# A two-layer hybrid model: the first layer's first two projections on x laid out by features, and the values' projection moved to second place

## The chip, the cores and the metric

The kernel runs on one NeuronCore of a Trainium2 chip, as one program with one launch. The metric is the device time of one execution in microseconds (us), the median of several runs. TensorE (PE) multiplies matrices into PSUM, PEld is its loading of the stationary operand, VectorE (DVE), ScalarE (ACT) and GpSimd (POOL) work element by element, and SyncE (SP) issues all DMA transfers from one queue, in order. Each engine works through its own queue in the order in which the program was written out.

## What is computed

The input x has 256 tokens of 1024 features. It passes through two hybrid layers (`layer0`, `layer1`), then a SwiGLU block, a mixing block and another SwiGLU block, all with residual sums. The part that the change touches is the head of a hybrid layer:

```python
def rmsnorm(x, g):
    xf = x.astype(jnp.float32)
    y = xf * lax.rsqrt(jnp.mean(xf * xf, axis=-1, keepdims=True) + EPS)
    return (y * g.astype(jnp.float32)).astype(x.dtype)
...
    p = split_columns(rmsnorm(x, norm_g) @ w_in)
...
    dq = rmsnorm(heads(p['dsa_q'], DSA_HEADS), dsa_q_g)
    dk = rmsnorm(heads(p['dsa_k'], DSA_HEADS), dsa_k_g)
    iq = heads(p['idx_q'], IDX_HEADS) * (IDX_DIM ** -0.5)
    iw = p['idx_w'] * (IDX_HEADS ** -0.5)
    topk = min(TOPK_MAX, s // 4)
    hd = dsa_sparse_attention(dq, dk, heads(p['dsa_v'], DSA_HEADS), iq, p['idx_k'], iw, rel_bias, topk)
```

The sparse attention scores every key with the index projections (idx_q, idx_k, idx_w), keeps the 64 best keys of each query, and does softmax attention of four heads over them with a relative bias. Two other branches (an mLSTM and a gated linear attention) run beside it on other columns of the same projection, and one output projection joins the three. The norm's factor of a token is one number for its row, so it can be multiplied into a projection's result instead of into x; the gain g belongs to the feature, so it has to be in x or in the weights beforehand.

## The kernel before

All weights are read from DRAM in units of 128 x 1024 f32 (512 KB), in the order in which the program uses them (362 units). `fetch` loads a unit into `raw` (3 buffers), then ACT casts it to float32r (`hi`, line 123) and DVE computes the rest (`lo` = raw - hi, line 124); the pool `ws` holds 5 such pairs. A projection does three matmuls for each product: hi with x's high part, hi with x's low part, lo with x's high part (`mm3`, line 156). `proj_a` puts tokens on the partitions (512 columns, 4 units, 48 matmuls of 128x512), `proj_b` puts features there (units of 24 matmuls of 128x256).

A layer calls its projections in a fixed order: dq (queries), iq (index queries), misc (index keys, gates), dk (keys), gq and gk (linear attention), dv (values), dz (gate of the sparse attention), gv, mv, mo and so on. Between the units `tick` steps through jobs, generators that issue the other work in pieces: `dsa_select` makes the scores `sc` and takes the 64 best of them on DVE in eight rounds, and at its end (line 552) turns them into a penalty, which POOL adds to the bias `pen` (line 554, four adds). `join(select)` stands after dz, so that `dsa_attend` starts with gv: the logits `dl` on PE (line 597), `lg` on DVE (line 600: dl, scaled, plus `pen`), the softmax (lines 625 to 633), and four steps later the transposes `pTp` of the first 128 tokens' probabilities on PE (line 232). The scheduler then lays all instructions out engine by engine, with the weight splits given a priority ahead of the other work.

The program's start is separate (`run`): x is loaded with tokens on the partitions, `normed` computes the factor r of each token (ACT squares, DVE, POOL), DVE multiplies x by r and by the gain, PE transposes the result (`xT`), ACT and DVE split it into the high and low part, and the first dq matmul follows. Four matmuls on zeros (`warm`) stand before. Other constants are loaded behind the first weights, and a strip of the bias table goes to DRAM and back (`bias_build`).

```python
        self.load_x(0)
        self.xn, fill = self.norm(gains[stages[0]])
        self.load_x(1)
...
            turns[0]()
            first = self.weights()
            turns[1]()
```

Of the kernel before, what the change touches and what calls it, by code (L numbers as in the profile page):

```python
# [34 lines left out]
class Net:  # L35
    def __init__(self, ctx, tc, a, out, dbg=None):
# [9 lines left out]
        self.operands()  # L46
        self.gap(pool("mid"), 96)
        self.t2 = pool("t2", 7)
# [5 lines left out]
        self.unit = 0  # L54
        self.jobs, self.ready, self.pins = [], [], None
        self.consts()
# [94 lines left out]
    def mm3(self, out, w, x, swap, first, last):  # L151

        (wh, wl), (xh, xl) = w, x
        for i, (ww, xx) in enumerate(((wh, xh), (wh, xl), (wl, xh))):
            lhsT, rhs = (xx, ww) if swap else (ww, xx)
            self.nc.tensor.matmul(out, lhsT=lhsT, rhs=rhs, start=first and i == 0, stop=last and i == 2)  # L156

# [22 lines left out]
    def rows(self, ps, x, k0, first, last, toks, w):  # L180

        for k in range(2):
            ww = [z[:, 512 * k:512 * (k + 1)] for z in w]
            for t in toks:
                xs = [z[:, k0 + k, P * t:P * (t + 1)] for z in x]
                self.mm3(ps[t], ww, xs, True, first and k == 0, last and k == 1)

    def proj_b(self, x, name, n=2):
# [40 lines left out]
    def transposes(self, srcs, name):  # L229
        ps = self.bank([P, len(srcs), P], name)  # L230
        for i, s in enumerate(srcs):
            self.nc.tensor.transpose(ps[:, i, :], s, self.ident)
        return ps

    def consts(self):
        nc, a = self.nc, self.a
        self.x = self.big.tile([P, 2, D], F32, tag="x", name="x")
        nc.sync.dma_start(self.ident, a["ident"])
        self.mhalf = self.const.tile([P, 16], F32, tag="mhalf", name="mhalf")
        nc.gpsimd.memset(self.mhalf, -0.5)  # L240

    def load_x(self, t):
        self.nc.sync.dma_start(self.x[:, t, :], self.a["x"][P * t:P * (t + 1)])

    def warm(self):

        nc = self.nc
        w = self.tmp([P, 512], "warm")
        nc.vector.memset(w, 0.0)
# [10 lines left out]
    def loads(self):  # L260
        nc = self.nc
        self.cols = self.held("cols")
# [3 lines left out]
        self.ones = self.const.tile([4, S], F32, tag="ones", name="ones")  # L266
        nc.gpsimd.memset(self.ones, 1.0)
# [17 lines left out]

    def norm(self, g_src):


        g = self.row_bc(g_src, D, "g_bc")
        self.x2 = self.big.tile([P, KT, 2, S], F32R, tag="x2", name="x2")  # L290
# [22 lines left out]
    def normed(self, t, g):  # L313
# [4 lines left out]
        sq = [nc.scalar.activation(xs[h], self.x[:, t, 512 * h:512 * (h + 1)], AF.Square, scale=1.0 / 32, accum_out=ss[:, h:h + 1]) for h in range(2)]  # L318
        r = self.small([P, 1], "r")
        nc.vector.scalar_tensor_tensor(r, ss[:, 0:1], EPS, ss[:, 1:2], ALU.add, ALU.add)  # L320
# [64 lines left out]


    def bias_build(self):

        nc, a = self.nc, self.a
        tab = self.tmp([32, 4], "tab")  # L390
        nc.sync.dma_start(tab, a["rel_bias"])
        hot = self.tmp([32, 512], "hot")
        nc.sync.dma_start(hot, a["hot"])
        yield
        yield
        ps = self.bank([4, 512], "strip")
# [11 lines left out]
    def layer(self, l):  # L408
        nc, a = self.nc, self.a
        x = self.xn  # L410
        yh = self.work([P, 16, S], "yh", dtype=F32R)
        yl = self.work([P, 16, S], "yl", dtype=F32R)
        self.y = (yh, yl)

        qs = self.t4([P, 2, 512], "qs")
# [41 lines left out]
        nc.gpsimd.memset(v1[:, :, :, 256:257], 1.0)  # L457
        hp = self.work([P, 2, D], "hp")

# [17 lines left out]

        gbc = self.row_bc(a["ml_norm_g"][l], D, "mlg")

        def zs(u, need):  # L480
# [13 lines left out]
        self.join(scores)  # L494
        self.start(self.gla_out(gvs, srg))
        h1 = head(1)
        outs(1)
# [66 lines left out]

    def dsa_q(self, t, ps, qs, qT, rq):
        nc = self.nc
        nc.scalar.copy(qs[:, t, :], ps)
        self.head_rms(ps.rearrange("p (h d) -> p h d", h=4), rq[:, t, :], 1.0 / 128, 128 ** -0.5)
# [504 lines left out]
    def run(self, stages):  # L1073
        a = self.a
        gains = {"layer0": a["norm_g"][0], "layer1": a["norm_g"][1], "ffn1": a["ffn1_norm_2"], "mix": a["mix_norm_2"], "ffn2": a["ffn2_norm_2"]}
        self.load_x(0)
        self.xn, fill = self.norm(gains[stages[0]])
        self.load_x(1)
        self.floor = self.tc.cur_priority
        self.warm()  # L1080
        with self.tc.manual_schedule(engines={mybir.EngineType.Activation, mybir.EngineType.DVE}):
            turns = [fill(t) for t in range(2)]
            turns[0]()
            first = self.weights()
            turns[1]()
        self.ready = [first]
        self.turn = None
        self.loads()
        self.start(self.bias_build())
# [42 lines left out]
def layouts(np, ins):  # L1132
# [18 lines left out]
    for l in range(2):  # L1151
# [5 lines left out]
        misc[96:100, l] = g("ml_b_i")[l]  # L1157
        units += pa(w, C_DQ) + pb(w, C_IQ, 512) + pb(m, 0, P) + pa(w, C_DK) + pb(w, C_GQ, 256) + pb(w, C_GK, 256)
        head = lambda h: pb(w, C_MLQ + 256 * h, 256) + pb(w, C_MLK + 256 * h, 256)
        units += pa(w, C_DV) + pb(w, C_DZ, 512) + pa(w, C_GV) + pa(w, C_MLV) + pa(w, C_MLO) + head(0) + pa(w, C_GR)  # L1160
        units += pa(w, C_MLV + 512) + head(1) + pa(w, C_MLO + 512) + head(2) + pa(w, C_MLZ) + head(3) + pa(w, C_MLZ + 512)
# [37 lines left out]
    for n, c in enumerate(LEVELS):  # L1199
# [14 lines left out]
    arrays = {  # L1214
        "x": g("x")[0], "w": np.stack(units), "cols": cols, "gwa": gwa,
        "rel_bias": g("rel_bias"),
# [34 lines left out]
```

## Time and profile before

| what | value |
|---|---|
| median of 3 runs | 1130.99 us (1130.78 to 1131.72) |
| profiled execution, own time | 1133.35 us |
| its span | 1131.6 us |
| TensorE's granted clock, mean of the span | 0.996 of full speed |
| busy share of the span: PE, PEld, DVE, ACT, POOL | 99%, 85%, 72%, 54%, 9% |
| DMA | 203.74 MB, mean 180 GB/s |

The span runs from the first to the last recorded instruction; 1.75 us of the execution's own time lie around it. Matmul ends are modelled, so a busy PE is one that never stood empty for long, not one at its peak.

### The profile page before, as it was taken

What the parts mean: (1) busy time and instruction counts of PE and PEld (TensorE: products, weight loads), DVE (VectorE), ACT (ScalarE), POOL (GpSimd) and SP (SyncE); (2) the same over time, 40 slices, a digit from 0 to 9 for tenths busy, and PEclk for the clock granted to TensorE, in tenths of its full rate; (3) what the DMA queues carried; (4) which work ended last, traced back from release to release, by engine and by line L of the source; (5) the groups of instructions that cost most, each with busy time, mean ns of one, the idle gap of its engine ahead of it and who ended that gap; (6) DMA issues with size and microseconds to landing.
All of it is one profiled execution on the core that took longest, in us unless ns stands there. A gap on an engine that the chain in (4) does not pass through costs nothing.

```text
span 1131.6 us, 16690 instructions
## 1 busy us (share of the span) xinstructions
PE 1118.4 (99%) x6330; PEld 962.3 (85%) x6330; DVE 810.8 (72%) x1233; ACT 616.3 (54%) x950; POOL 105.0 (9%) x136
## 2 busy tenths in 40 slices
PE   8999999999999999999999999999999999999997
PEld 5888889898898989899888888887888998888886
DVE  5688897786568879778747777646698676777743
ACT  4645854564465575456535555444566545555532
POOL 1111102121111210112100000000010001000000
PEclk8999999999999999999999999999999999999999
DMA  8846644455574654455557665666754566666662
GB/s 261 269 151 188 191 153 151 157 168 184 161 216 150 186 182 135 133 160 167 177 165 222 188 191 190 195 188 190 226 182 144 174 189 184 195 188 190 197 190 74
DMA packets 59464, 203.74 MB, mean 180 GB/s; under 512 B 6700, under 2 KB 9652, under 8 KB 59384
## 3 DMA queue, kind: packets, MB, share of 16 engines
q1 hardware_dynamic: 59384, 202.68, 58.3%
q8 instruction: 50, 0.82, 0.3%
q14 instruction: 30, 0.25, 0.1%
HBM read 201.46 MB, written 2.11 MB: 180 GB/s over the span
## 4 chain that ended last, share of the span: by engine, by line
PE 95%; DVE 3%; ACT 1%; DMA 1%; issue 0%; SPq 0%; POOL 0%; DVEq 0%; POOLq 0%; ACTq 0%
PE op L156 20%; PE fg L209 6%; PE fu L209 6%; PE mq L156 4%; PE mk L156 4%; PE mo L156 4%; PE mz L156 4%; PE mv L156 4%; PE fg L210 3%; PE fu L210 3%; PE gatep L209 3%; PE dq L156 2%; PE dz L156 2%; PE brp L156 2%; PE iq L156 2%; PE dk L156 2%
## 5 line engine op out<-in xcount | busy, mean ns | idle before, releaser
L124 DVE TENSOR_TENSOR lo<-raw,hi 128x1024 fp32r<-128x1024 f32 x359 | 443.1, 1236 | 217.1 <-ACT hi L123 216.1
L123 ACT CAST hi<-raw 128x1024 fp32r<-128x1024 f32 x362 | 379.0, 1048 | 371.6 <-PE op L156 91.8
L209 PE MATMUL fu<-x,hi 128*128 128x512 f32 x288 | 101.0, 394 | 0.0
L209 PE MATMUL fg<-x,hi 128*128 128x512 f32 x288 | 100.8, 394 | 0.0
L210 PE MATMUL fg<-x,lo 128*128 128x256 f32 x288 | 79.9, 277 | 0.0
L210 PE MATMUL fu<-x,lo 128*128 128x256 f32 x288 | 79.8, 277 | 0.0
L156 PE MATMUL op<-hi,hh 128*128 128x512 f32 x176 | 68.6, 390 | 0.0
L156 PE MATMUL op<-lo,hh 128*128 128x512 f32 x176 | 68.5, 389 | 0.0
L156 PE MATMUL op<-hi,hl 128*128 128x512 f32 x176 | 68.5, 389 | 0.0
L209 PEld LDWEIGHTS fg<-x,hi 128*128 128x128 f32 x288 | 54.0, 188 | 12.6
L209 PEld LDWEIGHTS fu<-x,hi 128*128 128x128 f32 x288 | 54.0, 188 | 12.5
L321 POOL TENSOR_TENSOR r<-r,mhalf 128x1 f32<-128x1 f32 x12 | 6.7, 555 | 528.5 <-DVE r L320 528.5
L210 PEld LDWEIGHTS fg<-x,lo 128*128 128x128 f32 x288 | 54.1, 188 | 0.1
L210 PEld LDWEIGHTS fu<-x,lo 128*128 128x128 f32 x288 | 54.1, 188 | 0.0
L156 PE MATMUL op<-hi,yh 128*128 128x512 f32 x128 | 51.1, 399 | 0.0
L156 PE MATMUL op<-lo,yh 128*128 128x512 f32 x128 | 50.0, 391 | 0.0
L156 PE MATMUL op<-hi,yl 128*128 128x512 f32 x128 | 49.9, 390 | 0.0
L156 PE MATMUL mq<-x,hi 128*128 128x256 f32 x256 | 48.2, 289 | 0.0
L156 PE MATMUL mk<-x,hi 128*128 128x256 f32 x256 | 46.8, 284 | 0.0
L209 PE MATMUL gatep<-x,hi 128*128 128x512 f32 x128 | 46.1, 403 | 0.0
L697 DVE SCALAR_TENSOR_TENSOR cacc<-pad,cols,cacc 128x256 f32<-128x256 f32 x96 | 41.0, 479 | 0.0
L156 PE MATMUL mv<-hi,x 128*128 128x512 f32 x128 | 40.7, 399 | 0.0
(361 smaller groups left out, 2598.7 us busy)
## 6 DMA issues: line engine op xcount, KB each, us to landing
raw<-in_w SPq DMA_DIRECT2D x362, 512.0 KB, 3.6
x<-in_x SPq DMA_DIRECT2D x2, 512.0 KB, 5.1
g_bc<-in_norm_g SPq DMA_DIRECT2D x2, 512.0 KB, 4.5
mlg<-in_ml_norm_g SPq DMA_DIRECT2D x2, 512.0 KB, 5.1
skew<-strips SPq DMA_DIRECT2D x4, 256.0 KB, 5.2
pen<-skew SPq DMA_DIRECT2D x8, 128.0 KB, 2.9
mb<-M SPq DMA_DIRECT2D x2, 512.0 KB, 4.3
g_bc<-in_ffn_norm SPq DMA_DIRECT2D x2, 512.0 KB
```

The lines of the kernel that those rows point to most:

```text
L123: a = nc.scalar.copy(hi, raw)
L124: b = (nc.gpsimd if pool else nc.vector).tensor_tensor(lo, raw, hi.bitcast(F32), ALU.subtract)
L156: self.nc.tensor.matmul(out, lhsT=lhsT, rhs=rhs, start=first and i == 0, stop=last and i == 2)
L209: nc.tensor.matmul(ps, lhsT=wh[:, ks], rhs=self.x2[:, k], start=k == 0, stop=False)
L210: nc.tensor.matmul(ps[:, 1, :], lhsT=wl[:, ks], rhs=self.x2[:, k, 0, :], start=False, stop=k == KT - 1)
L321: pw = nc.gpsimd.tensor_tensor(r, r, self.mhalf[:, 0:1], ALU.pow)
L697: nc.vector.scalar_tensor_tensor(acc[:, c, :], pad[:, c, 1 + i:1 + i + S], w(i), acc[:, c, :], ALU.mult, ALU.add)
```

## The change

In the first layer dq and dv no longer take the normed and transposed x. The host hands in x a second time, laid out by features (`xt`, 128 partitions x 8 x 256), and the gain by features (`g0`). ACT and DVE multiply `xt` by the gain and split it in one step each (`scaled`), into the still unused tiles yh and yl; dq and dv run on that. The norm's factor r is multiplied into their results (`dsa_q`, `dvs`). The normed x, which all other projections need, is made while PE works on dq and dv: `spread` copies the gain row to all partitions with two matmuls on PE, and `later` issues the transposes between the units of dv. Six units are loaded and split by a list written out by hand. In both layers dv now stands second, right behind dq (the weights are stored in that order too), and its result goes into the slot that the norm's gain row and `mlg` also use, so that `mlg` is loaded later. The warming matmuls become three.

```diff
+    def first(self, yh, yl, hp):
...
+            load = lambda u, c=slice(0, 1024): nc.sync.dma_start(raws[u][:, c], a["w"][u][:, c])
+            nc.sync.dma_start(g[0:1, :], a["norm_g"][0:1, :])
+            nc.sync.dma_start(g0, a["g0"])
+            halves = [slice(0, 512), slice(512, 1024)]
+            for u in range(4):
+                ks = slice(2 * u, 2 * u + 2)
+                nc.sync.dma_start(xt[:, ks, :], a["xt"][:, ks, :])
+                for c in halves if u == 0 else (slice(0, 1024),):
+                    load(u, c)
+            self.cols = self.held("cols")
+            self.load_x(0)
+            load(4)
+            nc.sync.dma_start(self.ident, a["ident"])
+            load(5)
+            self.load_x(1)
+            self.bias_load()
+            for u in range(6):
+                if u < 4:
+                    self.scaled(xg, xt, g0, (2 * u, 2 * u + 1))
+                for c in halves if u == 0 else (slice(0, 1024),):
+                    self.split(*[z[:, c] for z in ws[u]], raws[u][:, c])
+                if u > 3:
+                    turns.append(fill(u - 4))
+                if u == 3:
+                    self.spread(g, w)
...
+    def spread(self, g, w):
...
-        for _ in range(4):
+        for _ in range(3):
             nc.tensor.matmul(ps, lhsT=w[:, :P], rhs=w, start=True, stop=True)
+        pg = [self.bank([P, 512], f"gb{h}") for h in range(2)]
+        for h in range(2):
+            nc.tensor.matmul(pg[h], lhsT=self.ones[0:1, 0:P], rhs=g[0:1, 512 * h:512 * (h + 1)], start=True, stop=True)
+        for h in range(2):
+            nc.scalar.copy(g[:, 512 * h:512 * (h + 1)], pg[h])
+
+    def scaled(self, out, x, g, ks):
+        for k in ks:
+            self.nc.scalar.mul(out[0][:, k, :], x[:, k, :], g[:, k:k + 1])
+            self.nc.vector.scalar_tensor_tensor(out[1][:, k, :], x[:, k, :], g[:, k:k + 1], out[0][:, k, :].bitcast(F32), ALU.mult, ALU.subtract)
...
-        self.proj_a(x, "dq", lambda t, ps: self.start(self.dsa_q(t, ps, qs, qT, rq)))
+        self.proj_a(xg, "dq", lambda t, ps: self.start(self.dsa_q(t, ps, qs, qT, rq, raw)))
+        if raw:
+            self.loads()
+        dv = self.proj_a(xg, "dv")
+        dvs = self.big.tile([P, D], F32, tag="bc", name="dvs").rearrange("p (t d) -> p t d", t=2)
+        for t in range(2):
+            if raw:
+                nc.scalar.mul(dvs[:, t, :], dv[t], self.rs[t])
+            else:
+                nc.scalar.copy(dvs[:, t, :], dv[t])
...
-        dv = self.proj_a(x, "dv")
-        dvs = self.t4([P, 2, 512], "dvs")
-        for t in range(2):
-            nc.scalar.copy(dvs[:, t, :], dv[t])
```

On PE, at the program's start, this stood in the queue (`xT` are the transposes of the normed x, `dq_197` and `dq_198` the two token halves of dq's sum):

```order
L252 MATMUL warm<-warm 128x512 x4
L232 MATMUL xT<-ident,xs_116 128x128 x4
L232 MATMUL xT<-ident,xs_117 128x128 x4
L232 MATMUL xT<-ident,xs_126 128x128 x4
L232 MATMUL xT<-ident,xs_127 128x128 x4
L156 MATMUL dq_197<-hi,x_104 128x512 x2
```

and this stands there now (`gb` are the two matmuls that spread the gain row, `yh` and `yl` the parts of the scaled x):

```order
L316 MATMUL warm<-warm 128x512 x3
L319 MATMUL gb_187<-g_bc,ones 128x512
L319 MATMUL gb_188<-g_bc,ones 128x512
L157 MATMUL dq_223<-hi,yh 128x512
L157 MATMUL dq_223<-hi,yl 128x512
L157 MATMUL dq_223<-lo,yh 128x512
```

The 16 transposes have moved behind dq, into the units of dv.

On DVE, in the first layer, this stood between the end of the selection (`sc`, line 552, two rows of W further up) and the logits `lg`:

```order
L576 TENSOR_TENSOR gg<-cols 128x1 x2
L124 TENSOR_TENSOR lo<-raw,hi 128x1024 x3
L448 SCALAR_TENSOR_TENSOR sdz<-th_dz,dz 128x512
L124 TENSOR_TENSOR lo<-raw,hi 128x1024 x2
L448 SCALAR_TENSOR_TENSOR sdz<-th_dz,dz 128x512
L124 TENSOR_TENSOR lo<-raw,hi 128x1024
L600 SCALAR_TENSOR_TENSOR lg<-dl,rq,pen 128x128 x4
```

and this stands there now, from the selection's last row on:

```order
L632 TENSOR_SCALAR sc<-sc 128x384
L767 SCALAR_TENSOR_TENSOR W<-mb,cdT,tri 128x256
L768 SCALAR_TENSOR_TENSOR W<-mb,cdT,tri 128x128
L663 TENSOR_TENSOR gg<-cols 128x1 x2
L125 TENSOR_TENSOR lo<-raw,hi 128x1024
L530 SCALAR_TENSOR_TENSOR sdz<-th_dz,dz 128x512
L687 SCALAR_TENSOR_TENSOR lg<-dl,rq,pen 128x128
L125 TENSOR_TENSOR lo<-raw,hi 128x1024
L687 SCALAR_TENSOR_TENSOR lg<-dl,rq,pen 128x128 x3
```

Four of the six weight splits between the selection and the first `lg` have gone from there, one of the two sdz has moved ahead of `sc`, and one split now stands inside the four `lg`. The second layer's rows moved in the same way.

On SP, the first loads were these:

```order
L238 DMA ident<-in_ident 128x128
L243 DMA x<-in_x 128x1024
L283 DMA g_bc<-in_norm_g 128x1024
L243 DMA x<-in_x 128x1024
L119 DMA raw<-in_w 128x1024 x3
```

and are these now (`hp` is the tile in which `xt` lands):

```order
L272 DMA g_bc<-in_norm_g 1x1024
L273 DMA g_110<-in_g 128x8
L277 DMA hp<-in_xt 128x512
L271 DMA raw<-in_w 128x512 x2
L277 DMA hp<-in_xt 128x512
L271 DMA raw<-in_w 128x1024
L277 DMA hp<-in_xt 128x512
L271 DMA raw<-in_w 128x1024
L277 DMA hp<-in_xt 128x512
L271 DMA raw<-in_w 128x1024
L331 DMA cols<-in_cols 128x186
L251 DMA x<-in_x 128x1024
```

The weights of dq now share the head of the queue with quarters of `xt`, and x by tokens stands behind dq's weights.

## Rows read from the trace of the kernel before

**Rows 1.** The page: span, and the chain that ended last by engine.
```profile
span 1131.6 us, 16690 instructions
...
PE 95%; DVE 3%; ACT 1%; DMA 1%; issue 0%; SPq 0%; POOL 0%; DVEq 0%; POOLq 0%; ACTq 0%
```

**Rows 2.** Stretches of the start, PE alone: length, busy, granted clock, DMA share, GB/s.
```profile
7.40:12.60 5.20, 2.33 (x16) 1.00 1.03 395
12.90:19.40 6.50, 5.93 (x14) 0.50 0.89 236
```

**Rows 3.** Timeline of PE at the start: start, length, line, operation, instructions.
```profile
1.51 5.88 PE L252 MATMUL warm<-warm 128*128 128x512 f32 x8 [1.51 <-DVE warm L249]
...
24.66 1.02 PE L397 MATMUL strip<-hot,tab 32*4 32x512 f32 x2
```

**Rows 4.** Chain that ended last, first layer: start, length, engine and tile.
```profile
28.67 5.75 PE iq L156 x48
...
43.92 5.47 PE dk L156 x24
...
109.00 0.44 PE pTp L232 x4
```

**Rows 5.** The same chain in the second layer.
```profile
360.54 2.75 PE dv L156 x12
363.29 0.44 PE kTp L232 x4
...
372.43 11.51 PE dz L156 x96
...
398.48 0.44 PE pTp L232 x4
```

**Rows 6.** Timeline of ACT and SP at the start, and a wait of SP's.
```profile
5.09 0.63 ACT L318 ACTIVATE xs<-x 128x512 f32<-128x512 f32 x1 [3.02 <-DMA x<-in_x]
...
9.74 0.33 SPq L391 DMA_DIRECT2D tab<-in_rel_bias  x1
...
11.03 0.33 SPq L393 DMA_DIRECT2D hot<-in_hot  x1
...
SPq L393 <- DMA raw<-in_w: 0.9, 1, 0.9
```

**Rows 7.** The page's costliest groups: busy, mean ns of one, idle before.
```profile
L124 DVE TENSOR_TENSOR lo<-raw,hi 128x1024 fp32r<-128x1024 f32 x359 | 443.1, 1236 | 217.1 <-ACT hi L123 216.1
L123 ACT CAST hi<-raw 128x1024 fp32r<-128x1024 f32 x362 | 379.0, 1048 | 371.6 <-PE op L156 91.8
...
L697 DVE SCALAR_TENSOR_TENSOR cacc<-pad,cols,cacc 128x256 f32<-128x256 f32 x96 | 41.0, 479 | 0.0
```

**Rows 8.** Groups of ACT with shapes kept apart.
```profile
L823 ACT ACTIVATE X<-X 128x256 f32<-128x256 f32 x16 | 6.7, 418 | 0.2
```

**Rows 9.** Timeline of DVE, first layer, end of the selection to the softmax.
```profile
88.76 0.34 DVE L552 TENSOR_SCALAR sc<-sc 128x384 f32<-128x384 f32 x1
...
91.42 5.14 DVE L124 TENSOR_TENSOR lo<-raw,hi 128x1024 fp32r<-128x1024 f32 x3
96.49 0.67 DVE L448 SCALAR_TENSOR_TENSOR sdz<-th_dz,dz 128x512 f32<-128x512 f32 x1
...
103.81 1.12 DVE L600 SCALAR_TENSOR_TENSOR lg<-dl,rq,pen 128x128 f32<-128x128 f32 x4
107.79 0.69 DVE L633 TENSOR_TENSOR lg<-lg,srec 128x512 f32<-128x512 f32 x1
```

**Rows 10.** Timeline of POOL: the penalty's adds in the two layers.
```profile
89.19 5.16 POOL L554 TENSOR_TENSOR pen<-pen,sc 128x384 f32<-128x384 f32 x4 [15.73 <-DVE sc L552]
...
377.77 6.14 POOL L554 TENSOR_TENSOR pen<-pen,sc 128x384 f32<-128x384 f32 x4 [15.99 <-DVE sc L552]
```

**Rows 11.** Timeline of DVE, second layer, the same place.
```profile
377.34 0.35 DVE L552 TENSOR_SCALAR sc<-sc 128x384 f32<-128x384 f32 x1
...
379.04 2.04 DVE L124 TENSOR_TENSOR lo<-raw,hi 128x1024 fp32r<-128x1024 f32 x1
```

More of the change, by code (lines that the diff above doesn't have):

```diff
@@ L46, in __init__ @@
         self.operands()
-        self.gap(pool("mid"), 96)
+        self.gap(pool("mid"), 32)
         self.t2 = pool("t2", 7)
@@ L54, in __init__ @@
         self.unit = 0
-        self.jobs, self.ready, self.pins = [], [], None
+        self.jobs, self.ready, self.pins, self.turn = [], [], None, None
+        self.rs, self.pe_pin = [None, None], None
         self.consts()
@@ L155, in mm3 @@
             lhsT, rhs = (xx, ww) if swap else (ww, xx)
-            self.nc.tensor.matmul(out, lhsT=lhsT, rhs=rhs, start=first and i == 0, stop=last and i == 2)
+            mm = self.nc.tensor.matmul(out, lhsT=lhsT, rhs=rhs, start=first and i == 0, stop=last and i == 2)
+            if self.pe_pin is not None:
+                self.order([self.pe_pin, mm])
     def proj_a(self, x, name, by_token=None):
@@ L242, in load_x, with later @@
+        nc.gpsimd.memset(self.ones, 1.0)
     def load_x(self, t):
         self.nc.sync.dma_start(self.x[:, t, :], self.a["x"][P * t:P * (t + 1)])
-    def warm(self):
+    def first(self, yh, yl, hp):
+        nc, a = self.nc, self.a
+        g = self.big.tile([P, D], F32, tag="bc", name="g_bc")
+        self.xn, fill = self.norm(g=g)
+        g0 = self.const.tile([P, KT], F32, tag="g0", name="g0")
+        xt = hp.rearrange("p t (k s) -> p (t k) s", s=S)
+        xg = yh[:, 0:KT, :], yl[:, 0:KT, :]
+        w = self.tmp([P, 512], "warm")
+        E = mybir.EngineType
+        turns = []
+        with self.tc.manual_schedule(engines={E.Activation, E.DVE, E.SP}):
+            nc.vector.memset(w, 0.0)
+            nc.scalar.copy(self.small([4, 8], "pre", 1), self.ones[:, 0:8])
+            raws = [(self.wr.tile([P, 1024], F32, tag="raw", name="raw") if u < 3 else self.t4([P, 1024], "raw")) for u in range(6)]
+            ws = [[self.ws.tile([P, 1024], F32R, tag=z, name=z) for z in ("hi", "lo")] for _ in range(6)]
+            load = lambda u, c=slice(0, 1024): nc.sync.dma_start(raws[u][:, c], a["w"][u][:, c])
[23 more added lines that the diff above has]
+                    self.spread(g, w)
+        self.unit = 6
+        self.ready = [tuple(z) for z in ws]
+        self.floor = self.tc.cur_priority
+        def later():
+            for t in range(2):
+                for _ in range(4 - 3 * t):
+                    yield
+                turns[t]()
+            self.pe_pin = self.last_T
+        self.start(later())
+        return xg
@@ L284, in row_bc, with norm @@
         return t
-    def norm(self, g_src):
-        g = self.row_bc(g_src, D, "g_bc")
+    def norm(self, g_src=None, g=None):
+        if g is None:
+            g = self.row_bc(g_src, D, "g_bc")
         self.x2 = self.big.tile([P, KT, 2, S], F32R, tag="x2", name="x2")
@@ L318, in normed @@
         sq = [nc.scalar.activation(xs[h], self.x[:, t, 512 * h:512 * (h + 1)], AF.Square, scale=1.0 / 32, accum_out=ss[:, h:h + 1]) for h in range(2)]
-        r = self.small([P, 1], "r")
+        r = self.rs[t] = self.small([P, 1], "r")
         nc.vector.scalar_tensor_tensor(r, ss[:, 0:1], EPS, ss[:, 1:2], ALU.add, ALU.add)
@@ L384, in out_proj, with bias_load @@
         self.ready = [u[0] for u in units]
+    def bias_load(self):
+        self.tab = [self.tmp([32, n], f"tab{n}") for n in (4, 512)]
+        for t, z in zip(self.tab, ("rel_bias", "hot")):
+            self.nc.sync.dma_start(t, self.a[z])
     def bias_build(self):
[L389 to L395, printed above, removed]
+        nc = self.nc
+        for _ in range(6):
+            yield
+        tab, hot = self.tab
         ps = self.bank([4, 512], "strip")
@@ L413, in layer @@
         self.y = (yh, yl)
+        hp = self.work([P, 2, D], "hp")
+        raw = l == 0
+        xg = self.first(yh, yl, hp) if raw else self.xn
+        x = self.xn
         qs = self.t4([P, 2, 512], "qs")
@@ L417, in layer @@
         rq = self.small([P, 2, 4], "rq", 1)
-        self.proj_a(x, "dq", lambda t, ps: self.start(self.dsa_q(t, ps, qs, qT, rq)))
+        self.proj_a(xg, "dq", lambda t, ps: self.start(self.dsa_q(t, ps, qs, qT, rq, raw)))
[3 more added lines that the diff above has]
+        dvs = self.big.tile([P, D], F32, tag="bc", name="dvs").rearrange("p (t d) -> p t d", t=2)
+        for t in range(2):
+            if raw:
+                nc.scalar.mul(dvs[:, t, :], dv[t], self.rs[t])
+            else:
+                nc.scalar.copy(dvs[:, t, :], dv[t])
         iqT = self.t4([P, 4, S], "iqT")
@@ L457, in layer @@
         nc.gpsimd.memset(v1[:, :, :, 256:257], 1.0)
-        hp = self.work([P, 2, D], "hp")
         def values(u):
@@ L495, in layer @@
         self.start(self.gla_out(gvs, srg))
+        gbc = self.row_bc(a["ml_norm_g"][l], D, "mlg")
         h1 = head(1)
@@ L563, in head_rms, with dsa_q @@
         self.rsqrt(r, ss, scale, EPS, post)
-    def dsa_q(self, t, ps, qs, qT, rq):
+    def dsa_q(self, t, ps, qs, qT, rq, raw):
         nc = self.nc
-        nc.scalar.copy(qs[:, t, :], ps)
+        if raw:
+            for _ in range(2):
+                yield
+            nc.scalar.mul(qs[:, t, :], ps, self.rs[t])
+            ps = qs[:, t, :]
+        else:
+            nc.scalar.copy(qs[:, t, :], ps)
         self.head_rms(ps.rearrange("p (h d) -> p h d", h=4), rq[:, t, :], 1.0 / 128, 128 ** -0.5)
@@ L1075, in run @@
         gains = {"layer0": a["norm_g"][0], "layer1": a["norm_g"][1], "ffn1": a["ffn1_norm_2"], "mix": a["mix_norm_2"], "ffn2": a["ffn2_norm_2"]}
-        self.load_x(0)
-        self.xn, fill = self.norm(gains[stages[0]])
-        self.load_x(1)
         self.floor = self.tc.cur_priority
[L1080 to L1088, printed above, removed]
         self.start(self.bias_build())
@@ L1214, in layouts @@
     arrays = {
-        "x": g("x")[0], "w": np.stack(units), "cols": cols, "gwa": gwa,
+        "x": g("x")[0], "xt": g("x")[0].T.reshape(KT, P, S).transpose(1, 0, 2), "g0": g("norm_g")[0].reshape(KT, P).T, "w": np.stack(units), "cols": cols, "gwa": gwa,
         "rel_bias": g("rel_bias"),
```

21 lines of the change are left out of this document (9 added, 12 removed).

## The prediction

> **What bounds the kernel now.** I read the page first. The chain that ended last is 95% TensorE over a span of 1131.6 us [rows 1], so a saving counts only where PE stands empty or runs slowly, and a loss counts where PE is made to wait. Next I looked for those places by windows of PE. There is one, the program's start. From 7.40 to 12.60 us PE is busy for 2.33 of 5.20 us, because x has to land, be normed and be transposed. Then the granted clock, 1.00 until there, is 0.50 from 12.90 to 19.40 [rows 2]: 1.2 in place of 2.4 GHz, after a stretch in which PE had stood partly empty. That is 6.5 us at half speed, 3.25 us lost. Both together show in one number: the second projection, iq, starts at 28.67 [rows 4], though dq's 48 matmuls of 128x512 at full clock would need only 2 x 5.47 = 10.94 us (dk: 24 in 5.47, same rows).
>
> The second reading is DVE and POOL around the end of the selection, since the change moves a whole projection away from there. In the first layer `sc` is done at 89.1, POOL adds the penalty from 89.19 for 5.16 us [rows 10], DVE meanwhile makes weight splits, `lg` starts at 103.81 and the softmax's last product ends at 107.79 + 0.69 = 108.48 [rows 9]. PE wants the probabilities at 109.00 [rows 4]. So the lead is 0.5 us, and nothing waits yet.
>
> **The change part by part: the start.** Its own needs on PE, one after another, from the 7.39 at which the eight passes of warming end (1.51 + 5.88 [rows 3]):
>
> - Three warm matmuls and two `gb` are ten passes in place of eight. Two more at the full clock, 0.23 per pass of 512 columns in dk (5.47/24) and nearly twice that for an f32 pass; I take 0.43: dq could start at 8.25.
> - dq 10.94 and dv 10.94. dv is not new work: it goes from its later place (360.54 to 372.43 in the second layer holds dv and two groups of `kTp` of 0.44 [rows 5], so 11.0; I use 10.94 here).
> - 16 transposes in four groups, priced as four `pTp` groups of 0.44: 1.76. The strip, 1.02 [rows 3], stays ahead of iq.
>
> 8.25 + 10.94 + 10.94 + 1.76 + 1.02 = 32.9 for iq's start. Less dv, which had stood later, that is 22.0 against 28.67: 6.7 us gained. I take off 0.2 for the hand-overs between dq's units and keep **6.5**.
>
> This holds only if the weights are there. The first x half had landed by 5.05 before (`xs` starts at 5.09, released by that transfer), and two loads then followed each other at 9.74 and 11.03, 1.29 us per 512 KB at the rate of that stretch [rows 6]; 395 GB/s [rows 2] gives 1.33. With that pace the quarters of `xt` and the units land alternately: unit 0 at 5.6, unit 1 at 7.55, then 9.5 and 11.5; x and the small constants stand ahead of units 4 and 5, for which I get 14.3 and 15.8. ACT's cast (1.05) and DVE's split (1.24 [rows 7]) follow, with four `scaled` of 128x256 ahead of them for each of the first four units (two of 0.42 on ACT [rows 8], two of 0.48 on DVE [rows 7]). The six units would be ready at 6.95, 9.85, 11.9, 13.95, 16.6 and 20.1 (the last behind the norm's squares and products). PE wants them from 8.25 on, 2.74 apart: 8.25, 11.0, 13.7, 16.5, 19.2 and 21.9. The margins are 1.1 to 2.6 us. Thus I cost the loads, the scaling and the later norm at nothing: PE's own work on the earlier units hides them. If that cover is gone, a late unit costs its lateness once, as PE's later units are then waited for less. ACT's multiplication of dv by r has the instructions of the copy it replaces: nothing. The later load of `mlg` stands ahead of weight units in SP's queue and now waits for a slot that the sparse attention frees; the weights behind it are wanted some 14 us after that by my count of the order, so I cost it at nothing, with 0.5 as the other end.
>
> **The change part by part: the selection.** This is the term that speaks against the change. Between the start of the selection and the first `pTp` stood dv in both layers, 11.0 us of PE's work. It goes; the selection itself is DVE's work and gets no shorter. The following is on the clock of before with the selection held fixed (in the changed first layer everything here comes later by iq's 4.2).
>
> First layer: PE wants the probabilities at 109.00 - 11.0 = 98.0. DVE: `sc` ends at 89.1; one `sdz` of 0.67 now stands ahead of it, and 0.3 of that fits in front, so 89.4. The two W and gg follow as before (from 89.1 to 91.42 [rows 9]): 91.8. One split beside POOL, which shares that time: the three took 5.14, or 1.7 each; the one in the second layer, wholly beside POOL, 2.04 [rows 11]. Taking 2.0 to 2.3: 94.1. Then `sdz` 0.67, and the first `lg` at 94.8, which also needs POOL's first adds; POOL's four end at 89.8 + 5.16 = 94.95, so both are about even. `lg`, a split of 1.14 to 1.24 that now stands inside the four, three more `lg`: 97.0. From the start of `lg` to the end of the softmax it took 108.48 - 103.81 = 4.67, less `lg`'s own 1.12 [rows 9], 3.55: ready at 100.5. PE waits **2.5 us**. Bounds: 1.0, if the splits run without contention and the softmax loses its own split; 3.5, if each split takes 2.04.
>
> Second layer: wanted at 398.48 [rows 5] - 11.0 = 387.5. `sc` starts at 377.34 [rows 11]; 0.6 later for `sdz`, POOL's adds, 6.14 here from 377.77 [rows 10], end at 384.5; the last `lg` at 385.4; the softmax's 3.55: 389.0. PE waits **1.5 us**; bounds 0.5 and 2.5. What is queued behind `pTp` on PE are the products of the first 128 tokens and then mv and mo; they come later by the same amount and nobody makes it up, since PE is the bound to the end.
>
> **Sum.** -6.5 + 2.5 + 1.5 = -2.5. The profiled execution took 1133.35 of its own (span 1131.6 and 1.75 around it); the median shown is 1130.99. The difference is applied to the median: **1128.5**.
>
> **The clock in the two new waits.** The row at the start shows 1.00, then a stretch in which PE was busy for less than half, then 0.50 for 6.5 us [rows 2]. The new waits are half as long as that stretch, and PE is full before and behind them, so I expect 1.00 throughout. The Trainium skill, "TensorE: Matmul & The Clock Gate", section "HAM oscillation — how this bites in real kernels", speaks against the change here: waits between bursts of matmuls bring the throttle back, and half of the throttled time is lost. The trace agrees for the long gap of the start (0.50 behind it); no stretch of before shows it for a wait of 2 us. By that section the sum would hold a further loss per wait, as in rival C; without it, none.
>
> **Rivals.**
>
> - **B, no new wait.** DVE is ahead in both layers, for instance because the scheduler's splits there find their `raw` early and POOL's adds are shorter. For it: `lg` itself stood long after POOL had finished (94.4 against 103.81). Against it: 5.16 of adds and 3.55 of softmax behind `sc` are in series with the last `lg` of 0.28 between: 89.4 + 5.16 + 0.28 + 3.55 = 98.4, later than 98.0 even with nothing else. 1131.0 - 6.5 = 1124.5.
> - **C, the other side: the clock falls.** If PE's clock is halved behind a wait as it was at the start, 3.25 is lost each time: 1131.8 with one, 1135.1 with both. It decides once 2.5 more than the sum is lost, so one such fall is enough for no gain. For it: the only gap of before did this. Against: that gap was twice as long.
> - **D, small transfers.** Quarters and halves of 256 KB could each take as long as 512 KB (1.29): six of them, 6 x 0.65 = 3.9 us later for unit 3 and those behind it, against margins of up to 2.5: about 1.4 lost, 1129.9. For it: the rate of 395 GB/s was measured on 512 KB pieces only.
> - **E, heavier waits.** 4 us in each layer, as when splits of the next units stand ahead of the softmax beside POOL: -6.5 + 8 = +1.5, 1132.5.
>
> **How the numbers follow.** About 0.2%, 2.3 us, is what a measurement of this kernel can tell from no change. Chances: my forecast 0.60, B 0.13, C 0.09, D 0.10, E 0.08. The forecast's own range is 1126.5 to 1130.5 (bounds of the two waits), of which somewhat over half lies below 1128.7. Faster: 0.35 of the forecast and B, 0.48. Slower (above 1133.3): a half of E and the double case of C with some bad luck at the start, 0.10. The same: the rest, 0.42. The range reaches from B's 1124.3 to E's 1132.5; outside lie half of C, the worse half of E and a gain beyond B, under 2 in 10.
>
> **What would show it.** At the start: `warm` to 7.4, dq from about 8.2, no gap over 0.3 between its units, granted clock 1.00 up to iq, iq near 33. A dq that starts at 9.5 or later, or a unit's split that PE waits for, is D. At the selection: PE empty for some 2.5 us ahead of the first `pTp` of the first layer and 1.5 in the second, released by DVE's last product of the softmax; no gap is B, over 3.5 is E; a clock of 0.50 behind either is C. The prediction is wrong as a whole if a third place of waiting turns up, such as weights behind `mlg`, or if the start's gain is under 4 us.

## The result and the profile after

The change made the kernel slower: 1138.69 us in the median of 4 executions (1137.64 to 1139.99) against 1131.08 before, a ratio of 1.0065 with a 95% interval of 1.0052 to 1.0078. The forecast was 1128.5. The profiled execution took 1139.99, that of before 1133.35; their spans differ by 6.6 us. The page begins so (the chain's shares below the span):

```profile
span 1138.2 us, 16727 instructions
...
PE 85%; DVE 7%; issue 3%; ACT 1%; DMA 1%; POOL 1%; SPq 0%; DVEq 0%; POOLq 0%; ACTq 0%
```

The chain that ended last was 95% PE [rows 1]. Now it is 85%; 7% of it runs over DVE, the engine that PE waits for, and 3% is time in which nothing that the profile shows was waited for. Where PE waits, its timeline shows. First the start (start, length, and in brackets the idle time before with its releaser):

```profile
7.68 0.50 PE L157 MATMUL dq<-hi,yh 128*128 128x512 f32 x1
...
14.89 0.50 PE L157 MATMUL dq<-lo,yh 128*128 128x512 f32 x1 [0.29 <-DVE lo L150]
...
34.34 1.03 PE L239 MATMUL qTp<-ident,qs 128*128 128x128 f32 x8
35.13 0.48 PE L157 MATMUL iq<-x,hi 128*128 128x256 f32 x2
```

dq starts at 7.68, five microseconds earlier than before (12.62). dv follows, with the transposes and the strip between its units; `qTp`, which stood inside iq before, now precedes it. Then the waits:

```profile
78.59 0.50 PE L157 MATMUL dz<-x,hi 128*128 128x256 f32 x2 [1.55 <-DVE ks L668]
...
109.13 0.63 PE L239 MATMUL pTp<-ident,lg 128*128 128x128 f32 x4 [3.31 <-DVE lg L720]
...
401.68 0.63 PE L239 MATMUL pTp<-ident,lg 128*128 128x128 f32 x4 [1.16 <-DVE lg L720]
```

The two for `pTp` are the forecast ones; the one for dz, whose accumulator is freed by dk's `ks`, was not forecast (a second trace of the same kernel, e8, has 0.19 there). What they cost beyond their own length stands in the windows of PE (length, busy, granted clock, DMA share, GB/s):

```profile
8.00:20.00 12.00, 11.64 (x49) 1.00 1.02 378
20.00:34.30 14.30, 13.99 (x66) 1.00 0.59 197
102.00:109.00 7.00, 3.82 (x17) 1.00 0.57 157
110.40:113.40 3.00, 3.00 (x8) 0.50 0.67 197
404.00:407.00 3.00, 3.00 (x9) 0.50 0.68 212
26.10:28.80 2.70, 2.39 (x14) 1.00 0.00 0
```

At the start the clock is 1.00 throughout. Behind each wait for `pTp` it is 0.50 for three microseconds and somewhat more, with PE full: some 1.65 us lost each, as the positions of the next tiles show. In the last row the DMA engines move nothing: SP's queue stands still. Its timeline:

```profile
21.20 0.43 SPq L354 DMA_DIRECT2D g<-in_gla_norm_g  x1
28.91 0.33 SPq L120 DMA_DIRECT2D raw<-in_w  x1
```

and its waits from 15 to 40 us (us in all, times, longest):

```profile
SPq L120 <- DVE lo L125: 13.1, 6, 7.2
```

For 7.2 us the next weight load waits until DVE has split unit 6 and its buffer is free; that split stands on DVE behind the norm's products and the split of the transposed x. The weights behind it then come just in time, and on DVE this follows:

```profile
53.29 1.22 DVE L125 TENSOR_TENSOR lo<-raw,hi 128x1024 fp32r<-128x1024 f32 x1 [3.46 <-ACT hi L124]
54.44 0.48 DVE L511 TENSOR_SCALAR ms<-misc,cols 128x256 f32<-128x256 f32 x1
...
97.94 0.37 DVE L632 TENSOR_SCALAR sc<-sc 128x384 f32<-128x384 f32 x1
...
100.61 2.05 DVE L125 TENSOR_TENSOR lo<-raw,hi 128x1024 fp32r<-128x1024 f32 x1
...
108.29 0.69 DVE L720 TENSOR_TENSOR lg<-lg,srec 128x512 f32<-128x512 f32 x1
```

misc was ready on PE at 49.77. `ms`, with which the selection begins, stands in DVE's queue behind a split whose weights are late, and is made 4.7 us later (before: at once, 43.96 behind 43.92). At the end of the selection 3.3 us of that are left: `sc` at 97.94 lies 48.2 behind the end of misc, before 44.8 (88.76 [rows 9] and 43.92, where dk starts [rows 4]). From `sc` on all goes as forecast: one contended split of 2.05, `sdz`, one `lg`, a split, three `lg`, the softmax.

The account of the two spans, from the starts of the same tiles in both (dv's 11.0 taken into account): at the end of gk 5.0 us ahead; behind the wait for dz 3.2 ahead; behind the first `pTp` 0.3 behind; behind the clock's dip 1.9 behind; the first layer's end 2.1; the second layer's `pTp` 3.4; behind its dip 5.0; the end of the first SwiGLU block 6.8, and there it stays. The last step of 1.7 belongs to no wait and no dip: in this block the matmuls are 1 to 2% slower. The groups of PE by shape from 660 to 710 us, of the kernel before and then after:

```profile
L209 PE MATMUL fu<-x,hi 128*128 128x512 f32 x75 | 26.2, 394 | 0.0
```
```profile
L216 PE MATMUL fu<-x,hi 128*128 128x512 f32 x67 | 23.9, 399 | 0.0
```

394 against 399 ns for one, and since matmuls overlap, 5.55 against 5.65 us for a unit from start to start.

### The profile page after: what moved, and what is told of

The parts are those of the page before. It is cut to its first block, busy times and chain, and to the rows that moved or that the text cites. A ratio compares the mean times of both kernels' runs of the same rounds, so it can differ in the third digit from the quotient of the medians.

```text
span 1138.2 us, 16727 instructions
## 1 busy us (share of the span) xinstructions
PE 1121.7 (99%) x6332; PEld 963.5 (85%) x6332; DVE 812.7 (71%) x1242; ACT 621.7 (55%) x962; POOL 103.6 (9%) x136
## 4 chain that ended last, share of the span: by engine, by line
PE 85%; DVE 7%; issue 3%; ACT 1%; DMA 1%; POOL 1%; SPq 0%; DVEq 0%; POOLq 0%; ACTq 0%
PE op L157 20%; PE fg L216 6%; PE fu L216 6%; PE mq L157 4%; PE mk L157 4%; PE mo L157 4%; PE mz L157 4%; PE mv L157 3%; PE fg L217 3%; PE fu L217 3%; PE gatep L216 3%; DVE lo L125 2%; PE iq L157 2%; PE brp L157 2%; PE fg L157 2%
## 5 line engine op out<-in xcount | busy, mean ns | idle before, releaser
L125 DVE TENSOR_TENSOR lo<-raw,hi 128x1024 fp32r<-128x1024 f32 x353 | 434.5, 1231 | 211.0 <-ACT hi L124 210.0
L124 ACT CAST hi<-raw 128x1024 fp32r<-128x1024 f32 x356 | 372.9, 1048 | 366.5 <-PE op L157 90.8
L157 PE MATMUL mq<-x,hi 128*128 128x256 f32 x256 | 48.2, 289 | 0.0
```

The costliest lines, as they stand in the source:

```text
L124: a = nc.scalar.copy(hi, raw)
L125: b = (nc.gpsimd if pool else nc.vector).tensor_tensor(lo, raw, hi.bitcast(F32), ALU.subtract)
L157: mm = self.nc.tensor.matmul(out, lhsT=lhsT, rhs=rhs, start=first and i == 0, stop=last and i == 2)
```

## The experiments

Each execution's result gives its span S and its mean granted clock c. Time at half clock loses half of itself, so S(1 - c) is the most that the clock can have cost. It is not all cost: PE's last matmul ends some 7 us before the span does, and in each of the 17 traces the last 2.1 to 4.8 us of the span are at 0.50 with PE empty, here in the changed kernel's:

```profile
1134.50:1138.10 3.60, 0.00 (x0) 0.50 0.39 146
```

So 1.0 to 2.4 us of every S(1 - c) cost nothing, and differences of under 1 us between two means say little. The means over all executions follow; the kernel before has 1.9 to 3.0 us in five series (93 executions), of which this end is 1.3 and 1.5 in its two traces. The versions ran in several series, each beside the kernel before (its medians 1131.1 to 1132.6), so the ratios compare better than the medians:

| kernel | median us | ratio to before, 95% | S(1 - c), us |
|---|---|---|---|
| the changed kernel | 1138.69 | 1.0065 (1.0052 to 1.0078) | 6.0 |
| e8, the same again | 1138.37 | 1.0054 (1.0042 to 1.0066) | 7.5 |
| e4, before + dv second | 1139.40 | 1.0069 (1.0057 to 1.0080) | 5.1 |
| e3, early split | 1133.40 | 1.0014 (1.0006 to 1.0023) | 4.0 |
| e2, filled wait | 1134.34 | 1.0028 (1.0016 to 1.0040) | 2.8 |
| e1, later pTp | 1134.35 | 1.0026 (1.0018 to 1.0035) | 2.8 |
| e5, split + later pTp | 1137.81 | 1.0048 (1.0036 to 1.0060) | 6.6 |
| e9, both pTp later | 1140.00 | 1.0081 (1.0067 to 1.0095) | 7.4 |
| e6, e5 with dv second in the first layer only | 1133.22 | 1.0006 (0.9998 to 1.0015) | 4.0 |
| e10, e9 with dv second and pTp later in the first layer only | 1136.04 | 1.0033 (1.0020 to 1.0045) | 4.5 |
| e7, dv second in the first layer only | 1136.40 | 1.0034 (1.0022 to 1.0046) | 6.2 |
| e12, e7 + early split | 1132.36 | 1.0001 (0.9992 to 1.0009) | 4.6 |
| e11, e12 + mv as cover | 1131.57 | 0.9988 (0.9979 to 0.9997) | 3.4 |

**The move alone (e4).** The kernel before, with dv second:

```diff
         self.proj_a(x, "dq", lambda t, ps: self.start(self.dsa_q(t, ps, qs, qT, rq)))
+        dv = self.proj_a(x, "dv")
+        dvs = self.big.tile([P, D], F32, tag="bc", name="dvs").rearrange("p (t d) -> p t d", t=2)
...
-        dv = self.proj_a(x, "dv")
-        dvs = self.t4([P, 2, 512], "dvs")
```

> The kernel before, with nothing of the change but dv's place: second in both layers, its result in the slot of the gain row, mlg loaded later. The start is the old one. Theory 1 (the lost cover costs the same whatever the start): pTp waits some 2.5 us in the first and 1.2 in the second layer, the clock dips behind both, +3.7 of waits and +3.3 of clock, about 1138.1. Theory 3 (waits without a price in the clock): +3.7, 1134.8. Theory 2 (dv's place is innocent, the start or the tiles' places cost): within 1 us of before.

```profile
109.25 0.63 PE L232 MATMUL pTp<-ident,lg 128*128 128x128 f32 x4 [2.00 <-DVE lg L632]
...
401.55 0.63 PE L232 MATMUL pTp<-ident,lg 128*128 128x128 f32 x4 [1.16 <-DVE lg L632]
```

1139.40: by the medians the move alone costs all that the change costs, 8.2 us. The waits are 2.00 and 1.16, and the clock falls behind the first alone; `ms` comes 0.04 behind misc, so there is no late selection here. Theory 2, that dv's place is innocent, has fallen. The trace is of the fastest of the six executions (1136.34); its waits and its dip explain it, but the further 3 us of the median stand in no trace. The whole front of the change, with its start, then brings 0.7 (1139.40 to 1138.69), which the intervals cannot tell from nothing.

**The hole in SP's queue (e3).** Unit 6 is fetched ahead of the late transposes, its split pinned ahead of theirs:

```diff
-                turns[t]()
+                if t == 0:
+                    w, ab = self.fetch()
+                    self.ready.append(w)
+                    s = turns[t]()
+                    self.order([ab[1], s[0][1]])
+                else:
+                    turns[t]()
```

> The changed kernel, with weight unit 6 fetched ahead of the late transposes in the program and its split on DVE pinned in front of the split of x. In the changed kernel SP's queue stood from 21.7 to 28.9 us until that split freed a raw buffer, and the DMA engines were idle from 26 to 28.9. Theory 1 (that hole makes the units behind it late, and ms on DVE stands behind a late split, so the selection of the first layer ends 2.7 us late against PE): ms comes at once behind misc, the wait of dz (1.55) goes, the wait of pTp shrinks to about 2.2, 2.7 us less, about 1136.0. Rival (the selection is late because the skew and pen transfers now share the queue with the weights): ms stays late, no change.

The timelines of its DVE, SP and PE:

```profile
22.41 1.22 DVE L125 TENSOR_TENSOR lo<-raw,hi 128x1024 fp32r<-128x1024 f32 x1
```
```profile
23.66 9.27 SPq L120 DMA_DIRECT2D raw<-in_w  x4
```
```profile
105.92 0.66 PE L239 MATMUL pTp<-ident,lg 128*128 128x128 f32 x4 [2.46 <-DVE lg L726]
```

The split is done at 23.6, SP goes on at once, `ms` is 1.3 late (4.7 and, in e8, 3.2 in the changed kernel), and `pTp` waits 2.46, the forecast's 2.5. It starts at 105.92; in the two traces of the changed kernel it starts at 109.13 and 108.79. The wait for dz is gone, but it is as good as gone in e8 too, without this split. The clock still falls behind the wait for `pTp`. The median is 5.3 us below the changed kernel's, twice what was expected. The trace also has 5.55 us a unit in the first SwiGLU block, which is 1.7 of it. The rival (the skew and pen transfers, which are as many here) has fallen. With this split the start is worth 6.0 over e4 by the medians, and 3.8 at dk between the two traces (49.23 and 53.03).

**The clock (e2).** Work for nobody in the waits:

```diff
+                if t == 0:
+                    z = self.bank([P, 512], "fill")
+                    for _ in range((12, 4)[self.lay]):
+                        nc.tensor.matmul(z, lhsT=self.xn[0][:, 0, 0:P], rhs=self.x2[:, 0], start=True, stop=True)
                 tp = self.transposes([pr[:, h, P * b:P * (b + 1)] for h in range(4)], "pTp")
```

> The changed kernel, with 12 (first layer) and 4 (second layer) matmuls of 128x512 on data that nobody reads put in front of the first pTp: 2.7 and 0.9 us of work on PE inside waits of 3.31 and 1.16 us. Theory 1 (the clock falls because PE stands empty): pTp starts when it did, the granted clock stays at 1.00 behind it, 3.3 us less than the changed kernel, about 1135.4. Theory 3 (the clock falls for another reason): the dips stay, no change from 1138.7.

PE's timeline, and then the clock behind it in the windows:

```profile
104.36 2.88 PE L697 MATMUL fill<-x 128*128 128x512 f32 x12
107.85 0.63 PE L239 MATMUL pTp<-ident,lg 128*128 128x128 f32 x4 [0.61 <-DVE lg L725]
...
398.81 0.63 PE L239 MATMUL pTp<-ident,lg 128*128 128x128 f32 x4 [0.24 <-DVE lg L725]
```
```profile
108.00:112.00 4.00, 4.00 (x19) 1.00 0.76 221
399.00:406.00 7.00, 7.00 (x33) 1.00 0.76 256
```

The softmax is as late as it was (the filling and 0.61 make about the old wait), and the clock stays at 1.00. With work that computes nothing the kernel is 4.35 us faster. The mean of S(1 - c) falls from 6.0 to 2.8, as was expected for the two dips (3.3); the rest goes with the pace in the SwiGLU block, 5.55 again in this trace. Over all traces, the start left aside: behind each of 13 waits of PE between 2.00 and 4.83 us the clock fell to 0.50; behind six of 1.12 to 1.55 it fell once; behind those under 0.9 never. Behind the 13 it stayed there for some 3.4 us in seven cases and for twice that in six, and not by the length of the wait: 4.83 (e10) had the short dip, 2.13 (e5) the long one. A dip thus cost about 1.7 or about 3.4 us. In e8, the changed kernel's second trace, the first `pTp` had the long one, and a short one came at the start, where PE had been full since 1.5 us:

```profile
10.20:13.50 3.30, 3.30 (x9) 0.50 1.04 409
109.20:115.80 6.60, 6.60 (x16) 0.50 0.84 261
```

**More work ahead of `pTp` (e1, e5, e9, and e6, e10).** The steps between the softmax and its transposes, `3 + t` for the first (t = 0) and the next tokens, become `5 - t`, `4 - t` and 4:

```diff
-            for _ in range(3 + t):
+            for _ in range(5 - t):
                 yield
```

> The changed kernel, but the transposes of the first 128 tokens' probabilities (pTp) are issued two units later in both layers, so 5.5 us of mv's work stand ahead of them. Theory 1 (the lost cover makes PE wait 3.31 and 1.16 us for the softmax, and the halved clock behind each wait costs 1.65 more): both waits and both clock dips go, 7.8 us less than the changed kernel, about 1130.9 us. Theory 2 (the loss is a slower pace of the matmuls, from where the tiles now lie, and the waits are made up elsewhere): 1 us or less is gained. Theory 3 (the waits cost, the clock dips come from something else): the waits go, 4.5 us less, dips of the clock stay in the trace, about 1134.2.

e1: no wait for the first `pTp`, S(1 - c) at 2.8, 4.3 us gained of the 7.8. PE waits 0.81 and 0.68 at later places of the first layer, and this trace has the slow pace (5.65) in the second SwiGLU block.

> The kernel of e3 (early split), with pTp of the first 128 tokens one unit later in both layers (2.75 us of mv's work ahead of it) and the next tokens' pTp where it was. Waits left in e3: 2.46 in the first and 1.16 in the second layer, and 4.0 us of clock in the mean of its executions against 2.1 before. Theory 1 (waits and clock dips are the whole loss): both waits go and the clock's loss falls to some 2 to 2.5, about 5.3 us under e3's 1133.4, 1128.1 us, clear of the kernel before. Rival (the work moved later is waited for elsewhere, as the three waits of 0.8, 0.7 and 0.2 us in e1): 1130 or more.

> The kernel of e5, but the next tokens' pTp is moved one unit later as well (in e5 it stayed, its softmax began one unit later, and PE waited 3.68 and 2.13 us for it, with the clock lost behind). Theory 1: neither pTp waits, the clock's mean loss falls from e5's 6.6 to 2 to 3: 5.8 of waits and some 4 of clock under e5's 1137.8, about 1128.5. Rival (each move only hands the wait on, DVE and ACT being as late as PE is early): another wait of 2 us or more, 1131 or more.

The two waits of e5 and e9 in the first layer:

```profile
127.66 1.34 PE L239 MATMUL pTp<-ident,lg 128*128 128x128 f32 x8 [3.68 <-ACT X L916]
```
```profile
128.64 1.22 PE L957 MATMUL gp<-X 64*128 64x128 f32 x8 [4.49 <-DVE X L921]
```

Both expectations were wrong, the rival was right. In e5 the next tokens' softmax begins a unit later and its `pTp`, at its old place, waits 3.68; when that is moved too (e9), the gated linear attention's first products `gp` wait 4.49, because their last input `X` stands on DVE behind that softmax. The clock falls behind each. So a later consumer can hand the wait on, but it need not: in e1, where both `pTp` come two units later, DVE makes this `X` ahead of that softmax (whose maximum is `smax`), and `gp` starts at 124.65 with no wait. The rows of DVE in e1, and then the same `X` in e9, whose `smax` was at 119.97:

```profile
124.18 0.41 DVE L915 TENSOR_TENSOR X<-X,gqk 128x256 f32<-128x256 f32 x1
124.52 1.20 DVE L712 TENSOR_REDUCE smax<-lg 128x4 f32<-128x1024 f32 x1
```
```profile
128.17 0.42 DVE L921 TENSOR_TENSOR X<-X,gqk 128x256 f32<-128x256 f32 x1
```

What e1's places give together with e3's early split was not run.

> The kernel of e5, with dv back between gk and dz in the second layer (second only in the first layer). Theory 1 (with cover, dv's place in the second layer costs and gives nothing): the same as e5 within 1 us, about 1128. Rival (dv in second place costs something more there, DVE being busier with splits during the selection): 1 to 2 us less than e5.

> The kernel of e9 with dv back between gk and dz in the second layer, and there both pTp at their old places; the early split and the later pTp in the first layer stay. Theory 1: no wait for pTp in either layer, the same as e9 within 1 us, about 1128.5. Rival (dv's second place in the second layer costs more than its wait): 1 to 2 us less than e9.

Without dv's move in the second layer both are some 4 us faster than with it (1133.22 against 1137.81; 1136.04 against 1140.00, where the second layer's `pTp` are at their old places too), more than either theory expected: the second layer's handed-on waits, 2.13 and 3.28, go with their dips. In the first layer 3.44 and 4.83 stay.

**The second layer alone (e7), and the split with it (e12).**

```diff
+        if not raw:
+            values_dv()
         sdz = self.t4([P, 4, S], "sdz")
```

> The changed kernel, with dv back between gk and dz in the second layer alone; nothing else. Theory 1: the second layer's wait of 1.16 goes, and the dip behind it, which came in the changed kernel's trace but not in those of e3 and e4: 1.2 to 2.8 us less, about 1136.5. Theory 2 (place of tiles or the start alone): no change.

> The changed kernel with e3's early split and dv back in its old place in the second layer, nothing else: e11 without mv's move. Theory 1: the first layer's wait of about 2.5 and the dip behind it stay, the second layer's go: 1 to 2 us under e3's 1133.4, about 1131.8, level with the kernel before.

e7: 2.0 to 2.3 us less than the changed kernel, as expected. e12: 1132.36, level with the kernel before (1.0001); its first layer still waits 2.35 and dips. e7 and e12 differ by the early split alone: 4.0 us by the medians, of which 1.7 is the slow pace that e7's trace has and e12's has not.

**The cover given back (e11).** In the first layer mv, as large as dv, goes where dv had stood:

```diff
+        if raw:
+            values(0)
         sdz = self.t4([P, 4, S], "sdz")
...
-        values(0)
+        if not raw:
+            values(0)
         outs(0)
```

> The changed kernel with e3's early split and dv back in its old place in the second layer; in the first layer another projection of the same size, mv, is brought forward to where dv had stood, between gk and dz, so that the 11 us of PE's work between the start of the selection and pTp are there again, while dv keeps its second place and the start its gain. Theory 1 (what the change lost is this cover and what follows from it): no wait for pTp in either layer, the start some 5 us ahead of before, 1131.2 - 5 = 1126 to 1128, clear of the kernel before. Rival (the work behind, now one projection nearer to attention and its splits, waits instead: gp, gz or pTp of the next tokens, as in e5 and e9): 1131 or more.

```profile
115.73 0.60 PE L239 MATMUL pTp<-ident,lg 128*128 128x128 f32 x4
...
395.59 0.60 PE L239 MATMUL pTp<-ident,lg 128*128 128x128 f32 x4
```

No wait for either `pTp`; the largest of the layers is 0.88, for `gz`. 1131.57 beside 1132.55 of before in the same series: 0.9988 (0.9979 to 0.9997), the only version here that beats the kernel before, by 1 us and barely clear of its interval. The 1126 to 1128 expected were not reached; of the difference, 1.7 is the slow pace, which this trace has in the second SwiGLU block. The 5 us that the expectation took for the start were also too many: against e15, the kernel before once more, e11 is 0.6 ahead at the second layer's dq (303.03 against 303.66), with a short dip at its own start.

**The slow pace (e8, e13, e14, e15).** The changed kernel again; then the gap ahead of the temporaries at 96 bytes as before (changed kernel) and at 32 as after (kernel before); and the kernel before again:

```diff
-        self.gap(pool("mid"), 32)
+        self.gap(pool("mid"), 96)
```

> The changed kernel once more, unchanged, for more executions: about 1138.7. Theory 1: waits of about 3.3 and 1.2 us for pTp again, a mean loss of 5 to 6 us to the granted clock. The slower pace of the first SwiGLU block's matmuls (5.65 us for a unit against 5.55) was of that one execution: it need not come again.

> The changed kernel with the gap in front of the pool of temporaries at 96 bytes a partition, as before, in place of 32. In three traces with the changed start (the changed kernel twice, e7) the first SwiGLU block's units take 5.65 us in place of 5.55, some 1.7 us in all. If the place of the tiles behind the gap sets that pace: 5.55 in the first block and 1.7 less, about 1136.8. If not: 5.65 again or by chance, 1138.5.

> The kernel before with the gap at 32 bytes a partition as in the changed one, nothing else. If the gap sets the pace: 5.65 in a SwiGLU block and 1.7 more than before, about 1132.9. If not: 5.55 and no change from 1131.2.

> The kernel before, unchanged, for a second trace: 1131.2, and 5.55 us for a unit in both SwiGLU blocks as in its first trace; the start's clock dip of some 3 us in it again or not.

e8 has 5.65 in the first SwiGLU block again, so it goes with the program, and not with the one execution as was supposed. e13 has 5.55 there, but 5.65 in the second block and slower output projections (394 to 398 ns for a matmul in the median, 389 in the changed kernel): 1142.76, 1.0087 (1.0060 to 1.0113), which neither expectation had. So the gap does set a pace, and the old value is worse for the new layout. e14: 1132.82, 1.0005 (0.9996 to 1.0015), 5.55 in both blocks. e15: 1131.51, 5.55 in both. So the tiles' places move a pace of 1 to 2% between stages that the change doesn't touch. By what means stays open; the gap is not all of it, for e3, with the same pools and gap as the changed kernel, has 5.55 in both blocks.

## Why the prediction was wrong

**The clock.** "I expect 1.00 throughout", since the waits are half as long as the stretch at the start: this step failed, and in the trace it is the largest. There are dips of 1.65 us behind both waits, and in the mean of its executions the changed kernel has 3.9 us (4.9 in e8's series) more S(1 - c) than the kernel before. The comparison had misread its own stretch: the 5.20 us [rows 2] held several waits, the longest of them shorter than the 2.5 that was forecast:

```profile
11.48 1.38 PE L232 MATMUL xT<-ident,xs 128*128 128x128 f32 x8 [2.00 <-DVE xs L325]
```

So the trace of before did show a fall behind a wait of 2 us. Rival C had the mechanism, and its price of 3.25 each was about right for six of the 13 dips and twice too much for seven. e2 shows the cause: filled, the same waits leave the clock alone. The Trainium skill, "TensorE: Matmul & The Clock Gate", section "HAM oscillation — how this bites in real kernels", says that waits between bursts bring the throttle back. The waits that it works through are longer than the two forecast here, so the prediction's further loss for each of them went beyond that section; the traces decide, and they show the fall from 2.00 us on.

**The start's loads "at nothing".** The forecast followed each unit to its first use on PE and found them in time; they nearly are: PE stands empty for 0.4 of the 12 us of dq. It did not follow SP's queue, which for 7.2 us waits for one buffer, nor the instruction behind a late split on DVE, `ms`. e3 shows this: moved ahead, the split frees the buffer, and the selection is nearly on time. The hole made the first layer's loss 1.55 + 3.31 (0.19 + 3.36 in e8) in place of 2.5; with it mended the wait is 2.46. The wait for dz is also the third place of waiting that the prediction had named as a sign of being wrong as a whole.

**The start's gain.** 6.5 forecast, 5.0 measured at the end of gk between the two first traces. dq began 0.6 earlier than forecast, but took 12.1 us in place of 10.94, and the stretch of dv, transposes and strip 14.5 in place of 13.7, with idle pieces of 0.3. The larger error is in what was subtracted from: of the 6.5, 3.25 is the clock's dip of before [rows 2], and the kernel before does not always have it. Its second trace, e15, waits 0.63, 1.48 and 1.12 at the start, and the clock stays up:

```profile
12.90:19.40 6.50, 5.38 (x24) 1.00 0.89 255
```

There iq starts at 26.09 in place of 28.51, and the execution took 1131.25, close to the median. The first trace's took 1133.35, 2.4 more, so the sum took off the median a gain that was read from a dearer execution. Against e15 the changed start is 2.7 us ahead at dk (41.35 + 11.0 - 49.61), not 5. The changed start has its own dips, too: near 10 us, half as long as that of before and with PE full, in 8 of the 13 traces that have this start, with or without the early split, though not in the changed kernel's first.

**The waits for `pTp`.** Right in place, order and size: 2.00 and 2.46 (first layer without a late selection) for 2.5; 1.16 for 1.5. In the changed kernel itself the first is 3.31, within its bounds of 1.0 to 3.5.

**What was not in it.** The gap's new size stood in the diff and was not spoken of; the slow pace is 1.7 us. Together, between the two first traces: -2.5 + 1.5 (start) + 2.4 (first layer) - 0.3 (second) + 3.3 (clock) + 1.7 (pace) = 6.1, of the spans' 6.6; the rest is in pieces under 0.4, such as `gz` at 155.95.

## What to carry to other kernels

When work is taken from between a long chain on another engine and its consumer, the chain's lead is spent first; count that lead and add the clock to the price of every wait on PE, for here two waits of 4.5 us cost 3.3 more. Moving the consumer back can hand the wait to the next one (e5, e9) or not (e1), by the order on the engine that feeds both; other work of the same size in the vacated place took both waits away (e11). Follow a new start through the queue that feeds it and the instructions behind its late ones, not only to PE's first use. And before a stretch of one trace is counted as a gain, see in a second trace whether it is always there.

## What the runs showed of the hardware that was not expected

- The clock's dip needs no long wait: outside the start it came behind all 13 waits from 2.00 us on, cost about 1.7 or about 3.4 us, and work on data that nobody reads kept it away.
- The same program's dips differ from execution to execution, and at the start they come even with PE full; a single trace of a change of a few us can mislead (e4's own took 1136.3, its median is 1139.4).
- Matmuls at full clock and without waits ran at two paces, 5.55 and 5.65 us for a unit of the SwiGLU blocks, by program and by 64 bytes a partition of layout. The cause was not settled.
